# A decoder layer's weight products, 256 columns a matmul: one order of three products for each gate/up group

## Chip, cores and metric

One NeuronCore of a Trainium2 chip. The metric is the device time of one launch in microseconds (us), from first to last instruction with what little lies around them; lower is better.

## What is computed

A hybrid decoder layer on a residual stream h of 256 tokens by 2048 columns in float32. Every norm is an RMS norm with a gain, except the layer norm in the convolution.

```python
h = h + 0.5 * rms(swiglu(rms(h), w_gu[2048, 11264], w_down[5632, 2048]))      # FFN 1
z = rms(h) @ w_in[2048, 5120]                                                  # conv a, g; q, k, v
h = h + rms(concat(conv_group(a, g), moba_attention(q, k, v)) @ w_out)         # token mixing
h = h + rms(cross_attention(rms(h), rms(mem)))                                 # 4 heads, 256 memory rows
h = h + 0.5 * rms(swiglu(rms(h), w_gu, w_down))                                # FFN 2
```

With 256 tokens there is one MoBA block, so the attention is causal attention inside it.

## The kernel before

**Three products.** TensorE multiplies in float32r, a type of reduced precision. To keep float32 accuracy, each operand is split in two float32r parts, hi and lo, with value = hi + lo. A weight product w·x is then the sum of three matmuls that accumulate in PSUM: hi·xh, hi·xl and lo·xh. `Weights` (lines 96 to 220) loads weight tiles of 128 x 1024 on SP's DMA queue (4 buffers), makes hi on ScalarE (ACT, line 177 or 179, 4 buffers) and lo on VectorE (DVE, line 193 or 195, 3 buffers), ahead of use. `step` (line 318) issues this work for later tiles, then the matmuls of one tile, then pieces of `Background` work. All engine orders are the order of issue in the program; nothing is reordered later.

**Two layouts of a product.** In `proj_T` (line 418) the weights are the stationary operand, 128 of their columns for each load, and 256 tokens stream past them. A *region* is 256 columns of a PSUM bank, half a bank. In `proj` (line 429) 128 tokens are stationary and 512 weight columns stream, into a whole bank. Every matmul carries a weight load of its own, also where the same stationary operand comes twice running.

**Gate and up** (`gate_up`, line 622). A feed-forward layer has 22 groups g of 256 gate and 256 up columns; a group is 8 steps u, each one weight tile of two k-tiles (k = 2u + e) of the contraction. Groups 0 and 1 (`few`) use `proj_T`: 4 regions in 2 banks; for each k, hi·xh and hi·xl of region after region, then lo·xh of all four: 12 matmuls of 256 columns. The other 20 groups join the first two products: `xk` holds xh and xl side by side, so one matmul of 512 columns gives both partial sums in the two halves of a bank, and a matmul of 256 adds lo·xh to the second half:

```python
for ps, w in zip(pss, ws):
    nc.tensor.matmul(ps, hi[:, w], xk, start=k == 0, ...)             # L637, 512 columns, 4 banks
for ps, w in zip(pss, ws):
    nc.tensor.matmul(ps[:, 256:512], lo[:, w], xk[:, 0, :], ...)      # L639, 256 columns
```

That is 8 matmuls a k-tile, 4 banks a group. `queue_gate` (line 585) then queues background pieces: ACT copies one half of each bank (line 597) and DVE adds the other (line 598), for gate and for up; then the scale by 1/rms, silu, product, and the split of the result into hi and lo for the down product.

**Down** (line 483): two halves of the output columns, 44 k-tiles each, for each 2 token halves x 2 banks x 3 products with `proj` (lines 434, 436, 438), 512 columns each. The last 3 tiles of the second half are held back and done bank by bank. The output projection of the token mixing is the same function with 16 k-tiles. `in_group` (q, k) and `glu_group` (convolution) use `proj_T`, the v columns `proj`. The memory values (lines 1078 to 1080) have an own loop, with tokens stationary and 256 columns: per region xh·hi, xl·hi, xh·lo. During the token mixing DVE and GpSimd (POOL) also compute the 31 taps of the convolution (lines 747 and 758).

Of the kernel before, what the change touches and what calls it, by code (L numbers as in the profile page):

```python
# [14 lines left out]
P = 128  # L15
# [27 lines left out]
class Background:  # L43
    """Work that is issued a piece at a time between the weight tiles."""

# [12 lines left out]
    def urgent(self, pieces):  # L58
        """Each of the pieces in a step of its own, before all else that waits."""
        for fn, dve, act in reversed(pieces):  # L60
            self.main.appendleft(None)
            self.main.appendleft((fn, dve, act, 0.0))
# [33 lines left out]
class Weights:  # L96
    """The weights in the order of their use: loads, then the two float32r parts, ahead of the products."""

# [21 lines left out]
    def start(self):  # L120
        """The first rows and weights, in halves."""
        for i in range(2):
            self.raw[i] = self.pool.tile([P, 1024], F32, name="raw", bufs=RAW)
        for i, e in ((0, 0), (1, 0), (1, 1), (0, 1)):
            c = slice(e * 512, (e + 1) * 512)
            self.nc.sync.dma_start(self.raw[i][:, c], self.entries[i][0][:, c])
        key = self.entries[0][2]
        self.chunks[key] = c = self.chunk()
        self.hi[key], self.lo[key] = c[:, :, 0, :], c[:, :, 1, :]
        self.hi[1] = self.pool.tile([P, 1024], F32R, name="hi", bufs=HI)  # L130
        self.lo[1] = self.pool.tile([P, 1024], F32R, name="lo", bufs=LO)
        for i, e in ((0, 0), (1, 0), (1, 1), (0, 1)):
            k = i if i else key
            src, hi, g = list(self.parts(i, self.hi[k]))[e]
            lo = list(self.parts(i, self.lo[k]))[e][1]
            if g is None:
                self.nc.scalar.activation(hi, src, AF.Copy)
                self.nc.vector.tensor_tensor(lo, src, hi.bitcast(F32), ALU.subtract)
            else:
                self.nc.scalar.activation(hi, src, AF.Copy, scale=g)  # L140
                self.nc.vector.scalar_tensor_tensor(lo, src, g, hi.bitcast(F32), ALU.mult, ALU.subtract)
        self.raw.pop(0)
        self.raw.pop(1)
        self.n_raw = self.n_hi = self.n_lo = 2

    def parts(self, i, whole):
        """The pieces of an entry that have a gain each: (raw, part of the tile, gain)."""
        _, gains, _, rows, _ = self.entries[i]
# [75 lines left out]
def layer_kernel(ctx: ExitStack, tc: tile.TileContext, x, mem, eye, consts, smalls, post_g, xt, memt,  # L224
# [12 lines left out]
    def tmp():  # L237
        return ap.tile([P, 512], F32, name="tmp", bufs=TMP)
# [84 lines left out]

# [1 line left out]
    def rsqrt_of(ssq, n, eps_col, scale):  # L325
# [26 lines left out]
    class Rows:  # L352
        """Transposed float32r parts of [256, 2048] rows, and their 1 / rms."""

# [62 lines left out]

    def proj_T(regions, first, last, hi, lo, xk, parts_first=False):
        order = [(f, r) for f in range(2) for r in enumerate(regions)]
        if not parts_first:  # L420
            order = [(f, r) for r in enumerate(regions) for f in range(2)]
        for f, (j, (ps, o)) in order:
            nc.tensor.matmul(ps[:, o:o + 256], hi[:, j * P:(j + 1) * P], xk[:, f, :],  # L423
                             start=first and o == 0 and f == 0, stop=False, skip_group_check=True)
        for j, (ps, o) in enumerate(regions):
            nc.tensor.matmul(ps[:, o:o + 256], lo[:, j * P:(j + 1) * P], xk[:, 0, :],  # L426
                             start=False, stop=last, skip_group_check=True)

    def proj(pss, first, last, hi, lo, xk, t, n0=0):
        xh = xk[:, 0, t * P:(t + 1) * P]  # L430
        xl = xk[:, 1, t * P:(t + 1) * P]
        cols = [slice((n0 + n) * 512, (n0 + n + 1) * 512) for n in range(len(pss))]
        for ps, c in zip(pss, cols):
            nc.tensor.matmul(ps, xh, hi[:, c], start=first, stop=False)  # L434
        for ps, c in zip(pss, cols):
            nc.tensor.matmul(ps, xl, hi[:, c], start=False, stop=False)  # L436
        for ps, c in zip(pss, cols):
            nc.tensor.matmul(ps, xh, lo[:, c], start=False, stop=last)  # L438

# [3 lines left out]
    class Post:  # L443
        """Post-norm of [256, 2048] products and the update of the residual stream."""

# [20 lines left out]
        def early(self, t):  # L466
            """The sum over all but the last columns, as the bias of the square root."""
            s1 = scal()
            nc.vector.reduce_sum(s1, self.ssq[t][:, 0:3], axis=AX.X)
            self.bias = scal()  # L470
            nc.vector.tensor_scalar(self.bias, s1, self.factor / D, self.factor * RMS_EPS, ALU.mult, ALU.add)
# [11 lines left out]
    def down(nk, lhs, post, hook=None, tail=TAIL, keep=False):  # L483
        """Columns in two halves; the last tiles of the second go through the tokens one half after the other."""
        for hf in range(2):
# [3 lines left out]
            def mm(k, hi, lo):  # L489
                if hf == 1 and k >= nk - tail:  # L490
                    held.append((k, hi, lo))
                    return
                for t in range(2):
                    proj(pss[t], k == 0, k == nk - 1, hi, lo, lhs(k), t)

# [29 lines left out]
    def boundary(post, last, rows, fillers):  # L525
        """From the last products of the second token half to the first transposed columns of the next phase."""
        fillers = deque(fillers)
# [57 lines left out]
    def queue_gate(G, U, rows, hi_, lo_):  # L585
        """A pair of banks has the two partial sums of 128 columns in each, a single one the sums of 256."""
        box = []

        def add_parts(pss):
            s = tmp()  # L590
            box.append(s)
            if len(pss) == 1:
                nc.scalar.copy(s, pss[0])
                return
            for i, ps in enumerate(pss):
                c = slice(i * 256, (i + 1) * 256)
                nc.scalar.copy(s[:, c], ps[:, 256:512])  # L597
                nc.vector.tensor_tensor(s[:, c], ps[:, 0:256], s[:, c], ALU.add)  # L598

        def gate():  # L600
            add_parts(G)
            nc.vector.tensor_tensor(two(box[0]), two(box[0]), bc2(rows.rb), ALU.mult)

# [4 lines left out]
        def product():  # L608
            nc.vector.tensor_tensor(box[0], box[0], box[1], ALU.mult)
            make_hi(hi_, two(box[0]))  # L610

        bg.add(gate, dve=1.3, act=0.8)
        bg.cut()
        bg.add(silu, act=0.5, pool=1.2)
        bg.add(lambda: add_parts(U), dve=0.7, act=0.8)
        bg.cut()
# [5 lines left out]
    def gate_up(rows):  # L622
        hT = []
        for g in range(2 * NG):
            few = g < 2
            pss = [bank() for _ in range(2 if few else 4)]

            def mm(u, hi, lo):
                for e in range(2):
                    k = 2 * u + e  # L630
                    xk = rows.x(k)
                    if few:
                        proj_T(regions_of(pss), k == 0, k == KT - 1, hi[:, e * 512:], lo[:, e * 512:], xk, g == k == 0)
                        continue
                    ws = [slice(e * 512 + j * P, e * 512 + (j + 1) * P) for j in range(4)]
                    for ps, w in zip(pss, ws):
                        nc.tensor.matmul(ps, hi[:, w], xk, start=k == 0, stop=False, skip_group_check=True)  # L637
                    for ps, w in zip(pss, ws):
                        nc.tensor.matmul(ps[:, 256:512], lo[:, w], xk[:, 0, :], start=False, stop=k == KT - 1,  # L639
                                         skip_group_check=True)  # L640

# [4 lines left out]
            c = slice(2 * (g % 2), 2 * (g % 2) + 2)  # L646
            queue_gate(pss[:len(pss) // 2], pss[len(pss) // 2:], rows, hT[-1][:, c, 0, :], hT[-1][:, c, 1, :])
        return hT
# [16 lines left out]

# [1 line left out]
    mem_rows = []  # L667
# [13 lines left out]
    def kv_k(half):  # L681
        """Four pieces, one for each quarter of the contraction."""
        box = []
# [14 lines left out]

# [1 line left out]
    rows = Rows(h_rows, "x")  # L700
# [19 lines left out]

# [1 line left out]
    rows = Rows(h_rows)  # L722
# [287 lines left out]

# [1 line left out]
    rows = Rows(h_rows)  # L1012
# [132 lines left out]

# [1 line left out]
    bg.add(lambda: rows.tr(1, 1))  # L1147
# [110 lines left out]
```

## Time and profile before

| what | value |
|---|---|
| median of the two timed runs | 1979.92 us (1978.13 and 1981.71) |
| span of the profiled execution, first to last instruction | 1979.2 us |
| TensorE matmul busy | 1925.5 us, 97%, 11,034 matmuls |
| VectorE, ScalarE, GpSimd busy | 64%, 56%, 10% |
| mean granted TensorE clock | 0.997 |

The page gives the profiled execution's span; it lies between the two runs. PE is TensorE's matmuls, PEld its weight loads. A matmul's recorded duration holds the time that it spends in the array behind others, so the pace of a stream is read from the distance of the starts.

### The profile page before, as it was taken

What the parts mean: (1) busy time and instruction counts of PE and PEld (TensorE: products, weight loads), DVE (VectorE), ACT (ScalarE), POOL (GpSimd) and SP (SyncE); (2) the same over time, 40 slices, a digit from 0 to 9 for tenths busy, and PEclk for the clock granted to TensorE, in tenths of its full rate; (3) what the DMA queues carried; (4) which work ended last, traced back from release to release, by engine and by line L of the source; (5) the groups of instructions that cost most, each with busy time, mean ns of one, the idle gap of its engine ahead of it and who ended that gap; (6) DMA issues with size and microseconds to landing.
All of it is one profiled execution on the core that took longest, in us unless ns stands there. A gap on an engine that the chain in (4) does not pass through costs nothing.

```text
span 1979.2 us, 29214 instructions
## 1 busy us (share of the span) xinstructions
PE 1925.5 (97%) x11034; PEld 1675.8 (85%) x11034; DVE 1268.0 (64%) x1774; ACT 1098.7 (56%) x1793; POOL 204.8 (10%) x192
## 2 busy tenths in 40 slices
PE   8999999999999999887899999999999999999998
PEld 8888888888888889886797898988888888888886
DVE  5666666666544556999767576666666666644444
ACT  6655555555434646766465565755555555533433
POOL 0000000000000000768401000000000000000000
PEclk9999999999999999999999999999999999999999
DMA  8666666666655774344555653566666666666664
GB/s 289 187 190 191 191 192 190 189 189 192 210 191 187 256 244 141 130 149 139 166 165 169 214 179 120 181 191 191 188 189 191 191 191 192 212 188 187 189 189 142
DMA packets 102094, 369.62 MB, mean 187 GB/s; under 512 B 11456, under 2 KB 11712, under 8 KB 101184
## 3 DMA queue, kind: packets, MB, share of 16 engines
q1 hardware_dynamic: 100944, 361.00, 58.5%
q10 hardware_dynamic: 1008, 6.75, 0.9%
q8 instruction: 86, 1.41, 0.3%
q14 instruction: 56, 0.46, 0.1%
HBM read 365.61 MB, written 2.10 MB: 186 GB/s over the span
## 4 chain that ended last, share of the span: by engine, by line
PE 89%; DVE 6%; issue 2%; POOL 2%; ACT 1%; DMA 1%; SPq 0%; DVEq 0%; POOLq 0%; ACTq 0%
PE ps L637 30%; PE ps L639 15%; PE ps L438 11%; PE ps L434 10%; PE ps L436 10%; PE ps L423 7%; PE ps L426 3%; DVE lo L195 3%; DVE cv L747 2%; POOL cv L758 1%; PE ps L339 0%; DMA raw<-in_f_gu_dram 0%; ACT hi L179 0%; PE ps L1080 0%; PE ps L1078 0%
## 5 line engine op out<-in xcount | busy, mean ns | idle before, releaser
L195 DVE SCALAR_TENSOR_TENSOR lo<-raw,sm,hi 128x512 fp32r<-128x512 f32 (+1 forms) x830 | 636.4, 806 | 335.1 <-issue 249.3
L179 ACT ACTIVATE hi<-raw,sm 128x512 fp32r<-128x512 f32 (+1 forms) x830 | 576.4, 741 | 374.8 <-PE ps L637 220.9
L637 PE MATMUL ps<-ck,hi 128*128 128x512 f32 x2560 | 693.4, 393 | 0.0
L637 PEld LDWEIGHTS ps<-ck,hi 128*128 128x128 f32 x2560 | 434.5, 188 | 55.0
L193 DVE TENSOR_TENSOR lo<-raw,hi 128x1024 fp32r<-128x1024 f32 x216 | 265.4, 1230 | 282.4 <-PE ps L438 248.6
L639 PEld LDWEIGHTS ps<-ck,lo 128*128 128x128 f32 x2560 | 388.0, 188 | 53.8
L639 PE MATMUL ps<-ck,lo 128*128 128x256 f32 x2560 | 399.5, 278 | 0.0
L177 ACT ACTIVATE hi<-raw 128x1024 fp32r<-128x1024 f32 x216 | 228.7, 1060 | 297.2 <-PE ps L436 253.0
L438 PE MATMUL ps<-lo,ck 128*128 128x512 f32 x896 | 286.6, 397 | 9.1 <-DVE lo L195 7.8
L434 PE MATMUL ps<-hi,ck 128*128 128x512 f32 x896 | 286.7, 397 | 1.0 <-ACT ck L347 1.0
L436 PE MATMUL ps<-hi,ck 128*128 128x512 f32 x896 | 285.2, 396 | 0.0
L423 PE MATMUL ps<-ck,hi 128*128 128x256 f32 x1664 | 229.3, 283 | 9.5 <-ACT hi L140 6.2
L423 PEld LDWEIGHTS ps<-ck,hi 128*128 128x128 f32 x1664 | 210.2, 189 | 10.6 <-ACT hi L140 6.2
L438 PEld LDWEIGHTS ps<-lo,ck 128*128 128x128 f32 x896 | 168.1, 188 | 53.5 <-DVE lo L195 10.9
L436 PEld LDWEIGHTS ps<-hi,ck 128*128 128x128 f32 x896 | 168.3, 188 | 41.8 <-DVE ck L350 0.4
L434 PEld LDWEIGHTS ps<-hi,ck 128*128 128x128 f32 x896 | 168.0, 188 | 41.6 <-ACT ck L347 1.2
L606 POOL TENSOR_TENSOR tmp<-tmp,rb 128x512 f32<-128x512 f32 x44 | 58.2, 1322 | 1125.1 <-ACT tmp L605 1105.8
L426 PE MATMUL ps<-ck,lo 128*128 128x256 f32 x832 | 129.4, 283 | 23.3 <-DVE lo L195 23.3
L426 PEld LDWEIGHTS ps<-ck,lo 128*128 128x128 f32 x832 | 110.5, 188 | 28.3 <-DVE lo L195 28.2
L758 POOL TENSOR_TENSOR cv<-cv,cf 128x255 f32<-128x255 f32 (+14 forms) x120 | 106.3, 887 | 31.9 <-ACT cf L757 23.7
L747 DVE SCALAR_TENSOR_TENSOR cv<-yv,cf,cv 128x255 f32<-128x255 f32 (+14 forms) x120 | 85.1, 709 | 2.7
L598 DVE TENSOR_TENSOR tmp<-ps,tmp 128x256 f32<-128x256 f32 x160 | 60.1, 417 | 10.2 <-ACT tmp L597 10.2
(142 smaller groups left out, 925.8 us busy)
## 6 DMA issues: line engine op xcount, KB each, us to landing
raw<-in_f_gu_dram SPq DMA_DIRECT2D x351, 512.0 KB, 4.1
raw<-in_f_down_dram SPq DMA_DIRECT2D x176, 512.0 KB, 4.3
raw<-in_w_in_dram SPq DMA_DIRECT2D x80, 512.0 KB, 3.6
raw<-in_w_out_dram SPq DMA_DIRECT2D x32, 512.0 KB, 3.6
cf<-in_post_g_dram ACTq DMA_DIRECT2D x4, 1024.0 KB, 6.9
raw<-in_x_k_dram SPq DMA_DIRECT2D x8, 512.0 KB, 3.9
raw<-in_x_q_dram SPq DMA_DIRECT2D x8, 512.0 KB, 4.3
raw<-in_x_o_dram SPq DMA_DIRECT2D x8, 512.0 KB, 4.3
```

Of the source, the lines that this page charges most:

```text
L177: self.nc.scalar.activation(dst, src, AF.Copy)
L179: self.nc.scalar.activation(dst, src, AF.Copy, scale=g)
L193: self.nc.vector.tensor_tensor(dst, src, hi.bitcast(F32), ALU.subtract)
L195: self.nc.vector.scalar_tensor_tensor(dst, src, g, hi.bitcast(F32), ALU.mult, ALU.subtract)
L423: nc.tensor.matmul(ps[:, o:o + 256], hi[:, j * P:(j + 1) * P], xk[:, f, :], start=first and o == 0 and f == 0, stop=False, skip_group_chec ...
L426: nc.tensor.matmul(ps[:, o:o + 256], lo[:, j * P:(j + 1) * P], xk[:, 0, :], start=False, stop=last, skip_group_check=True)
L434: nc.tensor.matmul(ps, xh, hi[:, c], start=first, stop=False)
L436: nc.tensor.matmul(ps, xl, hi[:, c], start=False, stop=False)
L438: nc.tensor.matmul(ps, xh, lo[:, c], start=False, stop=last)
L637: nc.tensor.matmul(ps, hi[:, w], xk, start=k == 0, stop=False, skip_group_check=True)
L639: nc.tensor.matmul(ps[:, 256:512], lo[:, w], xk[:, 0, :], start=False, stop=k == KT - 1, skip_group_check=True)
L758: nc.gpsimd.tensor_tensor(cv[:, ct, s:], cv[:, ct, s:], pr[:, :S - s], ALU.add)
```

## The change

All products that were 512 columns wide become two of 256, the two partial sums of a gate/up group are accumulated in one region, and the order of the three products depends on the group's number (g % 11) or, in the down product, on the k-tile (k // 8 % 4). Groups with g % 11 = 6 (groups 6 and 17 of each feed-forward layer) go in 128 columns. The doc strings are removed as well. The order also changes where no mode is given: `proj_T` now does hi·xh, hi·xl, lo·xh region by region, where all lo·xh came last.

```diff
+    def proj_T(regions, first, last, hi, lo, xk, parts_first=False, mode=0):
+        rs = list(enumerate(regions))
+        order = [(r, i) for r in rs for i in range(3)]
+        if parts_first:
+            order = [(r, i) for i in range(3) for r in rs]
+        elif mode == 2:
+            order = [(r, i) for r in rs for i in (0, 2, 1)]
+        elif mode == 3:
+            order = [(rs[j], i) for j in (0, 2, 1, 3) for i in range(3)]
+        elif mode == 4:
+            order = [(rs[j + e], i) for j in (0, 2) for i in range(3) for e in range(2)]
+        elif mode == 5:
+            order = [(rs[j + e], i) for j in (0, 1) for i in range(3) for e in (0, 2)]
+        elif mode == 6:
+            for j, (ps, o) in rs:
+                for h in (0, 128):
+                    for i in range(3):
+                        nc.tensor.matmul(ps[:, o + h:o + h + 128], (hi, hi, lo)[i][:, j * P:(j + 1) * P],
+                                         xk[:, i % 2, h:h + 128], start=first and o == 0 and i == 0 and h == 0,
+                                         stop=last and i == 2, skip_group_check=True)
+            return
+        elif mode == 7:
+            order = [(r, i) for i in (0, 1) for r in rs] + [(r, 2) for r in rs[::-1]]
+        elif mode == 8:
+            order = [(r, i) for r in rs for i in range(2)] + [(r, 2) for r in rs[::-1]]
+        for (j, (ps, o)), i in order:
+            nc.tensor.matmul(ps[:, o:o + 256], (hi, hi, lo)[i][:, j * P:(j + 1) * P], xk[:, i % 2, :],
+                             start=first and o == 0 and i == 0, stop=last and i == 2, skip_group_check=True)
+
+    def proj(pss, first, last, hi, lo, xk, t, n0=0, mode=0):
+        xs = [xk[:, f, t * P:(t + 1) * P] for f in (0, 1, 0)]
+        if mode in (2, 3):
+            for n, ps in enumerate(pss):
+                for i, w in enumerate((hi, hi, lo)):
+                    for o in (0, 256):
...
+            return
+        for n, ps in enumerate(pss):
+            for o in (0, 256):
+                c = slice((n0 + n) * 512 + o, (n0 + n) * 512 + o + 256)
+                for i, w in enumerate((hi, hi, lo)):
+                    nc.tensor.matmul(ps[:, o:o + 256], xs[i], w[:, c], start=first and o == 0 and i == 0,
+                                     stop=last and i == 2, skip_group_check=True)
...
-                    proj(pss[t], k == 0, k == nk - 1, hi, lo, lhs(k), t)
+                    proj(pss[t], k == 0, k == nk - 1, hi, lo, lhs(k), t, mode=k // 8 % 4)
...
         def gate():
-            add_parts(G)
-            nc.vector.tensor_tensor(two(box[0]), two(box[0]), bc2(rows.rb), ALU.mult)
+            box.append(tmp())
+            nc.vector.tensor_tensor(two(box[0]), two(G), bc2(rows.rb), ALU.mult)
...
         def product():
-            nc.vector.tensor_tensor(box[0], box[0], box[1], ALU.mult)
+            nc.vector.tensor_tensor(box[0], box[0], U, ALU.mult)
...
-            few = g < 2
-            pss = [bank() for _ in range(2 if few else 4)]
+            pss = [bank() for _ in range(2)]
 
             def mm(u, hi, lo):
+                if g % 11 == 9 and u:
+                    for j, r in enumerate(regions_of(pss)):
+                        for e in range(2):
+                            k = 2 * u + e
+                            proj_T([r], k == 0, k == KT - 1, hi[:, e * 512 + j * P:], lo[:, e * 512 + j * P:], rows.x(k))
+                    return
                 for e in range(2):
                     k = 2 * u + e
...
+                    proj_T(regions_of(pss), k == 0, k == KT - 1, hi[:, e * 512:], lo[:, e * 512:], rows.x(k),
+                           g == k == 0, g % 11)
```

## Rows read from the trace of the kernel before

**Rows 1.** The page: span, busy time of each engine, TensorE's clock by slices.
```profile
span 1979.2 us, 29214 instructions
...
PE 1925.5 (97%) x11034; PEld 1675.8 (85%) x11034; DVE 1268.0 (64%) x1774; ACT 1098.7 (56%) x1793; POOL 204.8 (10%) x192
...
PEclk9999999999999999999999999999999999999999
```

**Rows 2.** Table by stretch: gate/up of FFN 1, its down, the convolution's stretch.
```profile
core 0: us, PE busy (x) PEld busy (x) DVE busy (x) ACT busy (x) POOL busy (x), PEclk, DMA share, GB/s
...
57.00:500.00 443.00, 443.00 (x2563) 388.54 (x2562) 291.19 (x457) 258.48 (x440) 27.93 (x21) 1.00 0.64 191
500.00:748.00 248.00, 248.00 (x1071) 199.39 (x1070) 126.88 (x135) 116.47 (x152) 1.30 (x1) 1.00 0.66 213
840.00:935.00 95.00, 77.78 (x593) 72.51 (x594) 93.44 (x109) 64.29 (x111) 72.72 (x78) 1.00 0.46 141
```

**Rows 3.** Chain of waits, 65 to 81 us, a wide gate/up group: start, us, what.
```profile
65.35 0.93 PE ps L637 x4
...
79.19 0.93 PE ps L637 x4
```

**Rows 4.** Chain of waits, 1270 to 1281 us, a narrow (few) gate/up group.
```profile
1270.44 0.94 PE ps L423 x8
...
1278.92 0.94 PE ps L423 x8
```

**Rows 5.** Chain of waits, 500 to 540 us, down product.
```profile
500.19 0.47 PE ps L436 x2
...
537.99 0.47 PE ps L436 x2
```

**Rows 6.** PE's timeline, 1195 to 1206 us: memory values, transposes: start, us, engine, line.
```profile
1194.79 0.28 PE L1078 MATMUL ps<-hi,ck 128*128 128x256 f32 x1
...
1197.06 0.28 PE L1080 MATMUL ps<-lo,ck 128*128 128x256 f32 x1
1197.17 0.60 PE L1051 MATMUL ps<-ident,cf 128*128 128x128 f32 x4
```

**Rows 7.** PE and PEld groups by line and shape: count, busy us, mean ns.
```profile
L637 PE MATMUL ps<-ck,hi 128*128 128x512 f32 x2560 | 693.4, 393 | 0.0
...
L423 PE MATMUL ps<-ck,hi 128*128 128x256 f32 x1664 | 229.3, 283 | 9.5 <-ACT hi L140 6.2 <-ACT hi L179 2.6 <-ACT ck L347 0.7
...
L1051 PE MATMUL ps<-ident,cf 128*128 128x128 f32 x16 | 2.4, 272 | 0.0
...
L423 PEld LDWEIGHTS ps<-ck,hi 128*128 128x128 f32 x1664 | 210.2, 189 | 10.6 <-ACT hi L140 6.2 <-ACT hi L179 2.8 <-ACT ck L347 0.9
...
L1051 PEld LDWEIGHTS ps<-ident,cf 128*128 128x128 f32 x16 | 1.8, 140 | 0.0
```

**Rows 8.** PE's timeline at 1052 us: one plain float32 product of 128 columns.
```profile
1052.12 0.39 PE L836 MATMUL ps<-cf 128*128 128x128 f32 x2
```

**Rows 9.** DVE and ACT groups, 57 to 500 us: the joining of the partial sums.
```profile
L598 DVE TENSOR_TENSOR tmp<-ps,tmp 128x256 f32<-128x256 f32 x76 | 28.6, 417 | 4.9 <-ACT tmp L597 4.9
...
L597 ACT COPY tmp<-ps 128x256 f32<-128x256 f32 x76 | 23.7, 360 | 0.0
```

**Rows 10.** Waits of PE, 755 to 1070 us: for whom, us in total, times, longest.
```profile
PE ps L426 <- DVE lo L195: 23.3, 24, 1.5
PE ps L438 <- DVE lo L195: 7.8, 6, 3.1
```

**Rows 11.** Chain of waits, 840 to 935 us: where it passes from DVE to PE.
```profile
869.75 1.66 DVE lo L195
871.40 0.04 issue
871.45 1.21 PE ps L426 x8
...
908.64 1.65 DVE lo L195
...
912.64 1.64 DVE lo L195
```

More of the change, by code (lines that the diff above doesn't have):

```diff
@@ L416, in h_rows @@
         return h[:, t, c * 512:(c + 1) * 512]
[L418 to L438, printed above, removed]
+    def proj_T(regions, first, last, hi, lo, xk, parts_first=False, mode=0):
[26 more added lines that the diff above has]
+                             start=first and o == 0 and i == 0, stop=last and i == 2, skip_group_check=True)
@@ new lines, in proj @@
+    def proj(pss, first, last, hi, lo, xk, t, n0=0, mode=0):
[10 more added lines that the diff above has]
+            for o in (0, 256):
+                c = slice((n0 + n) * 512 + o, (n0 + n) * 512 + o + 256)
+                for i, w in enumerate((hi, hi, lo)):
+                    nc.tensor.matmul(ps[:, o:o + 256], xs[i], w[:, c], start=first and o == 0 and i == 0,
+                                     stop=last and i == 2, skip_group_check=True)
@@ L587, in queue_gate @@
         box = []
[L589 to L598, printed above, removed]
         def gate():
-            add_parts(G)
-            nc.vector.tensor_tensor(two(box[0]), two(box[0]), bc2(rows.rb), ALU.mult)
+            box.append(tmp())
+            nc.vector.tensor_tensor(two(box[0]), two(G), bc2(rows.rb), ALU.mult)
         def silu():
@@ L608, in product @@
         def product():
-            nc.vector.tensor_tensor(box[0], box[0], box[1], ALU.mult)
+            nc.vector.tensor_tensor(box[0], box[0], U, ALU.mult)
             make_hi(hi_, two(box[0]))
-        bg.add(gate, dve=1.3, act=0.8)
+        bg.add(gate, dve=0.7)
         bg.cut()
         bg.add(silu, act=0.5, pool=1.2)
-        bg.add(lambda: add_parts(U), dve=0.7, act=0.8)
         bg.cut()
@@ L624, in gate_up @@
         for g in range(2 * NG):
-            few = g < 2
-            pss = [bank() for _ in range(2 if few else 4)]
+            pss = [bank() for _ in range(2)]
             def mm(u, hi, lo):
+                if g % 11 == 9 and u:
[4 more added lines that the diff above has]
+                    return
                 for e in range(2):
                     k = 2 * u + e
[L631 to L640, printed above, removed]
+                    proj_T(regions_of(pss), k == 0, k == KT - 1, hi[:, e * 512:], lo[:, e * 512:], rows.x(k),
+                           g == k == 0, g % 11)
             for u in range(8):
@@ L646, in gate_up @@
             c = slice(2 * (g % 2), 2 * (g % 2) + 2)
-            queue_gate(pss[:len(pss) // 2], pss[len(pss) // 2:], rows, hT[-1][:, c, 0, :], hT[-1][:, c, 1, :])
+            queue_gate(pss[0], pss[1], rows, hT[-1][:, c, 0, :], hT[-1][:, c, 1, :])
         return hT
```

## The prediction

> **What bounds the kernel now.** I read the page first. TensorE is busy for 1925.5 of 1979.2 us, VectorE for 64% and ScalarE for 56% [rows 1], and TensorE's clock stands at its upper level, 2.4 GHz, in every slice. So TensorE is the bound almost everywhere, and the question is what one matmul costs it. The table by stretch says where that doesn't hold: in gate/up and down PE is busy for the whole stretch, but from 840 to 935 us DVE is (93.4 of 95 us) and PE only for 77.8 [rows 2]. A busy PE says nothing of its pace, so I took the pace of each kind of stream from the distance between starts, in the chain of waits and in PE's timeline:
>
> - A wide gate/up group: the same piece of the chain starts at 65.35 and, five steps of two k-tiles later, at 79.19 us: 13.84 / 5 = 2.768 us a step [rows 3]. A step streams 24 x 256 columns, so 115.3 ns per 256 columns.
> - A narrow group (the first two, 256 columns a matmul): 8.48 us for six k-tiles of 12 matmuls, 117.8 ns a matmul [rows 4].
> - Down, 512 columns: 37.80 us for 27 rounds of six matmuls, 233.3 ns each, 116.7 per 256 columns [rows 5].
> - The memory values (tokens stationary, 256 columns, the three products of a region in a row): 20 starts from 1194.79 to 1197.06 us, 113.5 ns each [rows 6].
>
> So 256 columns cost between 113.5 and 117.8 ns in every stream, whatever the width of the matmul. At 2.4 GHz 256 columns alone are 106.7 ns. Each matmul has its own weight load: the counts of loads and matmuls are equal, 11,034 each [rows 1], also in the line that uses one stationary operand twice running (1,664 and 1,664) [rows 7]. At 256 columns the loads hide beside the streaming; the trace has no float32r product of fewer columns.
>
> **The change part by part.** The sum is made on the profiled execution's span, 1979.2 us, which lies 0.7 us below the median of the two timed runs (1979.92) and between them; I neglect that. The number of columns stays the same everywhere; what changes is in how many matmuls they come.
>
> *Groups 6 and 17, in 128 columns.* Four groups in all. A step has 2 k-tiles x 4 regions x 2 halves x 3 = 48 matmuls and 48 loads in place of 16. If only columns counted, one would take 113.5 / 2 = 57 ns; if the load is the pace, one can't be slower than a 256-column matmul with the same load, 118 ns. The nearest rows are the transposes: 128 columns and a load for each, four in a row in 0.60 us, of which the last one's own duration is 0.27, so (0.60 - 0.27) / 3 = 110 ns apart [rows 6, 7]. They stream half as many columns as the memory values and are hardly quicker, which looks like a load that sets the pace. The loads of float32r are recorded longer than theirs (189 against 140 ns), and still follow each other every 113.5 ns. I take 110. A step is 48 x 110 = 5.28 us instead of 2.768, that is +2.51 us, times 4 groups x 8 steps = 32: **+80.4 us**. Nothing hides it, since PE is busy there throughout. Bounds by the rows: 57 ns gives -1.0 us, 118 ns gives +92.7. Loads and splits for later tiles only get more time.
>
> The Trainium skill (TensorE: Matmul & The Clock Gate, "Back-to-back issue gap") speaks against so large a term: pairs of load and matmul shall sustain about 81 ns at 128 columns and 131 at 512. The trace doesn't bear the second figure out (233.3 ns [rows 5]), so I weigh the first little. By it the step would be 48 x 81 = 3.89 us and the term +35.9 in place of +80.4.
>
> *The other wide groups.* 2 x (20 - 2) = 36 groups, 288 steps, go from 16 matmuls to 24 of 256 columns. The nearest stream is that of the narrow groups, with the same operands: 24 x 117.8 = 2.827 us, +0.059 a step, **+17.0 us**. The other end is the pace of the memory values: 2.724 us a step, -12.7 us. The orders (modes 2 to 5, 7 to 9) lie somewhere between; no row tells them apart.
>
> *Down and the output projection.* Modes 0 and 1 have the very order of the memory values, with the same kinds of operand: 113.5 against 116.7 ns. Of the 512-column matmuls, 2 x 2 x 28 x 12 = 1344 in the feed-forward downs (k below 16 and from 32 on) and 2 x 16 x 12 = 384 in the output projection get this: 1728 x (233.3 - 227.0) = **-10.9 us**. The other 768 (modes 2 and 3) use one stationary operand twice running; I leave them at nothing, between -4.8 (at 227) and +1.8 us (at 235.6).
>
> *lo is needed sooner.* In `in_group` 16 matmuls ran before the first lo·xh, now two: 14 x 117.8 = 1.65 us less slack, in the v columns about 0.7. Where PE keeps pace this is covered, as lo is split two tiles ahead. From 840 to 935 us it isn't; between 755 and 1070 us PE waits for lo already, 30 times for 31.1 us [rows 10]. But the chain there runs in DVE, from one lo to the next in about 4.0 us [rows 11], against 2.83 us of matmuls, so waiting earlier costs nothing until the chain hands over to PE: at 871.45 us it continues with the 8 last lo products [rows 11], and will continue with 22 matmuls, 1.65 us more. Two such places: **+3 us**, between 0 and +8.
>
> *Gate without joining.* The copies and adds of halves go (76 of each in FFN 1's stretch, 23.7 us of ACT and 28.6 of DVE [rows 9]), and a group holds 2 banks, not 4. Neither engine is the bound there (DVE 291 of 443 us [rows 2]), so this gives nothing; it covers the change of order. DVE now reads gate and up from PSUM, in operations that it did before from SBUF, equally off the path.
>
> Sum: 80.4 + 17.0 - 10.9 + 3 = +89.5, **2069 us**. With the ends of the small terms and 109 to 118 ns for the narrow matmuls this case alone runs from about 2030 (+78.8 - 12.7 - 15.7) to 2102 us.
>
> **Rivals.**
> 1. *The array sets the pace in 128 columns as well* (the other side). Then a narrow matmul costs 57 ns, and the sum is -1.5 + 17.0 - 10.9 + 3, +8: 1987 us, no slower than can be measured. For it: no row shows a float32r load as a limit. Against: the transposes' 110 ns. The place is groups 6 and 17; below (39.6 - 9.1) / 32 = 0.95 us more a step, 78 ns a matmul, the change stays within 2%. Faster by over 2% it is only if the orders also run below every pace seen.
> 2. *A narrow product costs twice what I take*, because float32r in 128 columns is done as plain float32. A plain float32 product of 128 columns shows as two matmuls (0.39 - 0.27) = 0.12 us apart [rows 8], some 224 ns for the pair: 48 x 224 = 10.75 us a step, +255 us, 2244 us in all. For it: nothing in the kernel before is both float32r and narrower than 256. Against: plain float32 is two matmuls at 256 columns too, so type and not width decides.
> 3. *Waiting for lo becomes the path in the convolution's stretch.* If each of the 30 waits grew in full, 24 x 1.65 + 6 x 0.7 = 44 us come on top in place of 3: 2110 us. Against: after its lo PE needs 22 x 0.118 = 2.6 us of a DVE period of 4.0.
>
> **How the numbers follow.** The forecast has 0.75; rival 1 0.09; rival 2 0.11; rival 3 0.05. The range, 2020 to 2120 us, holds the forecast and rival 3; rivals 1 and 2 are left out. A measurement tells 2%, 39.6 us, from no change. Slower by more: the forecast, rivals 2 and 3, and 0.01 of rival 1, 0.92. Within: 0.06 of rival 1. Faster: its last 0.02.
>
> **What would show it.** PE has 11,034 + 2784 (each 512 of the tokens-stationary products split) + 36 x 16 x 4 + 4 x 16 x 16 = 17,146 matmuls. In the table by stretch group 6 should take some 42 us and its neighbours 22.6; starts in it 110 ns apart. A group 6 of 22 us is rival 1, of 86 us rival 2. Down should run at 113.5 ns where k is below 16, an unsplit group's neighbours at 117.8. The copies of halves are gone, PE's idle time is as before, and its waits for lo are longer but as many. The prediction is wrong if the narrow matmuls are under 100 or over 125 ns apart, or if orders differ by more than the 4 ns between the known paces.

## The result, and the profile after

| | us |
|---|---|
| before, median of 2 runs | 1979.92 (1978.13 to 1981.71) |
| after, median of 2 runs | 2083.83 (2080.97 to 2086.69) |
| after, profiled execution | 2080.97, span 2079.2 |
| ratio after to before | 1.0525, 95% interval 1.0505 to 1.0546 |

The change makes the kernel 5% slower; the forecast was 2069 us, the range 2020 to 2120.

The page, in the order of [rows 1]:

```profile
span 2079.2 us, 41201 instructions
...
PE 2026.0 (97%) x17146; PEld 2015.2 (97%) x17146; DVE 1214.4 (58%) x1614; ACT 1053.3 (51%) x1625; POOL 203.9 (10%) x192
...
PEclk9999999999999999999999999999999999999999
```

TensorE is still the bound and, slice by slice, still at its upper clock level (0.996 on average). There are 17,146 matmuls, as counted ahead, and as many loads. Weight loads are now busy for 97% of the span, against 85%: with fewer columns behind each load, there is almost no time without one.

The table by stretch, with the columns of [rows 2]. The stretches are gate/up group 3 of FFN 1, the narrow group 6, group 14 of FFN 1 and group 3 of FFN 2 (both in the order of group 3), FFN 1's down, and the convolution's stretch:

```profile
76.61:98.37 21.76, 21.76 (x195) 21.76 (x194) 13.32 (x19) 11.76 (x18) 1.30 (x1) 1.00 0.61 193
141.89:184.71 42.82, 42.82 (x386) 42.82 (x385) 13.11 (x19) 11.82 (x18) 1.27 (x1) 1.00 0.34 111
343.06:365.67 22.61, 22.61 (x194) 22.61 (x193) 13.21 (x19) 11.80 (x18) 1.29 (x1) 1.00 0.56 186
1351.71:1374.33 22.62, 22.62 (x195) 22.62 (x193) 13.21 (x19) 11.79 (x18) 1.30 (x1) 1.00 0.58 185
544.00:796.00 252.00, 252.00 (x2140) 251.95 (x2139) 126.56 (x132) 116.11 (x148) 1.29 (x1) 1.00 0.64 210
890.00:985.00 95.00, 78.20 (x614) 74.48 (x613) 93.51 (x110) 62.88 (x109) 71.16 (x76) 0.98 0.45 144
```

Three things are to be seen. The narrow group takes 42.8 us, where groups 5 and 7 beside it take 21.8 and 22.7; DVE and ACT do the same work in it, and the DMA share falls from 0.6 to 0.34, so it is TensorE alone that needs the time. Groups 3 and 14 have the same order of the three products and the same 192 matmuls, yet differ by 0.85 us; the same group 3 in FFN 2 differs from itself in FFN 1. And the convolution's stretch looks as it did: DVE 93.5 of 95 us, PE 78.

The paces come from the chain of waits, as before: start, us, what, and how many matmuls. Group 3, group 6, groups 9 to 11, FFN 1's down (lines 463 and 456 are two of its orders), the output projection of the mixing, and that of the attention:

```profile
75.97 22.10 PE ps L445 x195
...
142.05 42.83 PE ps L436 x384
...
251.94 24.15 PE ps L445 x205
...
559.94 29.68 PE ps L463 x252
589.62 10.48 PE ps L456 x89
...
1129.96 40.12 PE ps L463 x354
...
1257.92 12.12 PE ps L463 x101
```

By division: 113.3 ns a matmul in group 3; 42.83 us / 384 = 111.5 ns in the narrow group; 117.8 ns in groups 9 to 11; 117.8 in down, in both orders; 113.3 in one output projection and 120.0 in the other.

Stage by stage, from each stage's first matmul to the next's, in the traces of both kernels: gate/up 1 537.4 against 493.4 us (+44.1), gate/up 2 541.7 against 490.0 (+51.7), the downs 252.05 against 249.7 and 248.6 against 246.2 (+4.8), the output projection 100.3 against 101.15 (-0.8), the stages of the mixing before it -1.1, the attention's output projection +1.2. This adds up to the difference of the spans, 100 us, but for 0.1. Gate/up 2 loses 7.6 us more than gate/up 1: its groups 2 to 5 ran at 117.8 ns instead of 113.3 (3.4 us), and its groups 0 and 1 took 1.5 us more than in before, where those of FFN 1 took 2.6 less. The granted clock was 0.66 from 1280 to 1285 us, where gate/up 2 starts, and 1.00 at the same place in before (1234 to 1239 us).

### The profile page after: what moved, and what is told of

Its sections match the earlier page's. It is cut to its first block, busy times and chain, and to the rows that moved or that the text cites. A ratio compares the mean times of both kernels' runs of the same rounds, so it can differ in the third digit from the quotient of the medians.

```text
span 2079.2 us, 41201 instructions
## 1 busy us (share of the span) xinstructions
PE 2026.0 (97%) x17146; PEld 2015.2 (97%) x17146; DVE 1214.4 (58%) x1614; ACT 1053.3 (51%) x1625; POOL 203.9 (10%) x192
## 4 chain that ended last, share of the span: by engine, by line
PE 89%; DVE 5%; issue 2%; POOL 1%; ACT 1%; DMA 1%; SPq 0%; DVEq 0%; POOLq 0%; ACTq 0%
PE ps L445 49%; PE ps L463 21%; PE ps L456 9%; PE ps L436 8%; DVE lo L195 3%; DVE cv L757 2%; POOL cv L768 1%; DMA raw<-in_f_gu_dram 1%; PE ps L339 0%; ACT hi L179 0%; PE ps L1090 0%; PE ps L1088 0%; PE ps L1089 0%; DVE h L506 0%; DVE lo L193 0%
## 5 line engine op out<-in xcount | busy, mean ns | idle before, releaser
L445 PE MATMUL ps<-ck,hi 128*128 128x256 f32 x6272 | 1054.4, 280 | 8.0 <-ACT hi L140 6.8
L445 PEld LDWEIGHTS ps<-ck,hi 128*128 128x128 f32 x6272 | 915.2, 188 | 9.1 <-ACT hi L140 6.8
L445 PE MATMUL ps<-ck,lo 128*128 128x256 f32 x3136 | 775.4, 281 | 24.1 <-DVE lo L195 24.1
L445 PEld LDWEIGHTS ps<-ck,lo 128*128 128x128 f32 x3136 | 545.6, 189 | 29.0 <-DVE lo L195 29.0
L463 PE MATMUL ps<-hi,ck 128*128 128x256 f32 x2560 | 453.0, 281 | 1.3 <-ACT ck L347 1.0
L463 PEld LDWEIGHTS ps<-hi,ck 128*128 128x128 f32 x2560 | 392.7, 190 | 2.0 <-ACT ck L347 1.2
L463 PE MATMUL ps<-lo,ck 128*128 128x256 f32 x1280 | 360.1, 281 | 9.0 <-DVE lo L195 7.1
L463 PEld LDWEIGHTS ps<-lo,ck 128*128 128x128 f32 x1280 | 241.6, 189 | 10.6 <-DVE lo L195 8.4
L436 PE MATMUL ps<-ck,hi 128*128 128x128 f32 x1024 | 171.5, 275 | 0.0
L456 PE MATMUL ps<-hi,ck 128*128 128x256 f32 x1024 | 162.6, 281 | 0.0
L436 PEld LDWEIGHTS ps<-ck,hi 128*128 128x128 f32 x1024 | 155.5, 192 | 0.0
L436 PE MATMUL ps<-ck,lo 128*128 128x128 f32 x512 | 140.9, 275 | 0.0
L456 PEld LDWEIGHTS ps<-hi,ck 128*128 128x128 f32 x1024 | 139.4, 190 | 0.1
L456 PE MATMUL ps<-lo,ck 128*128 128x256 f32 x512 | 102.0, 281 | 0.0
L436 PEld LDWEIGHTS ps<-ck,lo 128*128 128x128 f32 x512 | 98.3, 192 | 0.0
```

The costliest lines, as they stand in the source:

```text
L436: nc.tensor.matmul(ps[:, o + h:o + h + 128], (hi, hi, lo)[i][:, j * P:(j + 1) * P], xk[:, i % 2, h:h + 128], start=first and o == 0 and i ...
L445: nc.tensor.matmul(ps[:, o:o + 256], (hi, hi, lo)[i][:, j * P:(j + 1) * P], xk[:, i % 2, :], start=first and o == 0 and i == 0, stop=last ...
L456: nc.tensor.matmul(ps[:, o:o + 256], xs[i], w[:, c], start=first and o == 0 and i == 0, stop=last and i == 2, skip_group_check=True)
L463: nc.tensor.matmul(ps[:, o:o + 256], xs[i], w[:, c], start=first and o == 0 and i == 0, stop=last and i == 2, skip_group_check=True)
```

## The experiments

**Without the narrow groups.** Groups 6 and 17 get the default order in 256 columns, the rest stays as after.

```diff
-                           g == k == 0, g % 11)
+                           g == k == 0, 0 if g % 11 == 6 else g % 11)
```

> The changed kernel with groups 6 and 17 in 256 columns too. Theory (pace kept from what came before): the narrow groups give back 4 x (42.8 - 22.6) = 81 us, and since nothing interrupts the stream after group 1, groups 6 to 21 of FFN 1 and its first down half keep the pace of groups 1 to 5; at 113.3 ns that is another 15 to 20 us, so about 1985 us, at 117.8 ns 2003 us. Rival (the order of the products sets the pace): 2003 us, groups 1 to 5 at 113.3 ns and groups 7 to 10 at 117.8 ns again.

Measured: 1995.33 us (1993.26 to 2002.59), ratio to before 1.0086, interval 1.0063 to 1.0109. So without the four narrow groups 2083.8 - 1995.3 = 88 us of the 104 are gone. By themselves they cost 4 x (42.83 - 22.61) = 81. The rest is the net of changes in stretches whose code was not touched. In the chain of waits, gate/up of FFN 1, then FFN 1's down and FFN 2's:

```profile
199.95 40.16 PE ps L445 x341
...
559.99 35.47 PE ps L456 x313
595.47 4.65 PE ps L463 x41
...
1799.90 26.97 PE ps L456 x229
1826.87 13.19 PE ps L463 x112
```

FFN 1's down now runs at 113.3 ns a matmul (it ran at 117.8 in after) and takes 243.45 us in place of 252.05; FFN 2's stays at 117.8. And all gate/up groups from 2 on run at 117.8, also those that ran at 113.3. The same instructions have two paces. Neither expectation held: with every order at 117.8 ns in both layers, the order doesn't set the pace, and down didn't keep the pace of the gate/up ahead of it.

**The narrow groups alone.** Before, with groups 6 and 17 in 128 columns and nothing else.

```diff
+            narrow = g % 11 == 6
+            pss = [bank() for _ in range(2 if few or narrow else 4)]
...
+                    if narrow:
+                        for j, (ps, o) in enumerate(regions_of(pss)):
+                            for c in (0, 128):
+                                for i in range(3):
+                                    nc.tensor.matmul(ps[:, o + c:o + c + 128], (hi, hi, lo)[i][:, ws[j]],
+                                                     xk[:, i % 2, c:c + 128],
...
```

> The kernel before with only groups 6 and 17 in 128 columns (512-column matmuls everywhere else). If the narrow groups are the cost by themselves, each takes 42.8 us in place of 22.1, +83 us, some 2063 us, with 111.5 ns between starts. If the cost depended on the 256-column streams around them, less.

Measured: 2062.96 us, 83 above before. In its chain of waits the narrow group stands among wide ones:

```profile
144.46 0.47 PE ps L649 x4
144.93 42.83 PE ps L641 x384
187.75 0.98 PE ps L647 x4
```

The same 42.83 us as in after, so the price depends neither on the neighbours' width nor on their pace.

**Other widths.** Group 6 comes in four matmuls of 64 columns, group 17 in one of 192 and one of 64 (as many loads as 128 + 128).

```diff
-                for h in (0, 128):
+                for h, n in cuts:
...
+                           [(0, 64), (64, 64), (128, 64), (192, 64)] if g < 11 else [(0, 192), (192, 64)])
```

> The changed kernel with group 6 in 64 columns a matmul and group 17 in 192 and 64 by turns. If the weight load sets the pace, starts are about 111 ns apart in both: group 6 takes 96 x 8 x 0.111 = 85 us and group 17 the same 42.8 us as with 128 and 128. If columns plus a fixed cost set it (111.5 = 57 + 55), group 6 takes 96 x 8 x 0.083 = 64 us, and group 17 shows two distances, some 140 and 83 ns.

Measured: 2304.91 us. Group 17, from the chain of waits:

```profile
535.61 42.80 PE ps L436 x384
```

192 + 64 columns take what 128 + 128 take, 111.5 ns on average. Columns with a fixed cost would give the same sum, so the single distances have to tell the two apart, in TensorE's timeline:

```profile
540.34 0.27 PE L436 MATMUL ps<-ck,lo 128*128 128x192 f32 x1
540.45 0.33 PE L436 MATMUL ps<-ck,hi 128*128 128x64 f32 x2
540.61 0.28 PE L436 MATMUL ps<-ck,lo 128*128 128x64 f32 x1
540.73 0.45 PE L436 MATMUL ps<-ck,hi 128*128 128x192 f32 x2
```

The last matmul of a run of three is followed after 0.11 us where it has 192 columns (540.34), and after 0.12 where it has 64 (540.61); columns with a fixed cost would make that 0.14 and 0.08. The single starts in the trace say the same: 111 to 115 ns in either width, and only behind the first matmul of each run 173 (192 columns) and 49 (64), together as much as two of the others. Group 6 agrees at first: 64 columns start 111.7 ns apart, as 128 do, and not the 83 of the rival. So the load, not the columns, sets the pace. The Trainium skill (TensorE: Matmul & The Clock Gate, "LDWEIGHTS (loading the stationary operand)") gives a load the number of stationary columns over 1.2 GHz, 106.7 ns for 128; 111.5 ns are 5% more.

Then group 6 shows something else, in TensorE's timeline:

```profile
147.46 0.39 PE L436 MATMUL ps<-ck,hi 128*128 128x64 f32 x2
...
150.81 0.39 PE L436 MATMUL ps<-ck,hi 128*128 128x64 f32 x2
...
151.20 0.61 PE L436 MATMUL ps<-ck,hi 128*128 128x64 f32 x2
...
152.48 0.61 PE L436 MATMUL ps<-ck,hi 128*128 128x64 f32 x2
```

From 147.46 to 150.81 us 30 matmuls start 111.7 ns apart, from 151.20 to 152.48 six start 213 ns apart. The table by stretch has the granted clock (the columns of [rows 2]):

```profile
143.00:150.00 7.00, 7.00 (x64) 7.00 (x62) 3.66 (x6) 2.67 (x4) 0.00 (x0) 1.00 0.51 170
...
200.00:300.00 100.00, 100.00 (x471) 100.00 (x470) 7.67 (x11) 6.67 (x10) 0.00 (x0) 0.50 0.08 27
322.00:340.00 18.00, 18.00 (x155) 18.00 (x154) 9.97 (x15) 8.67 (x14) 1.30 (x1) 1.00 0.52 179
```

The granted clock fell from 1.00 to 0.50 (1.2 GHz), while TensorE was busy without a gap, and came back once the stream had 256 columns again. The group took 160.2 us, where 85 were expected. Loads follow the clock: 471 matmuls in 100 us are 212 ns each. In 128 columns this did not happen; the clock of the narrow groups stands at 1.00 in after and in the run before this one.

**One order, different starts.** All gate/up groups have the default order in 256 columns; the first k-tile of group g begins with g // 2 + 1 matmuls that are split in two of 128.

```diff
-        for (j, (ps, o)), i in order:
+        for n, ((j, (ps, o)), i) in enumerate(order):
+            if n < cut:
+                for h in (0, 128):
+                    nc.tensor.matmul(ps[:, o + h:o + h + 128], (hi, hi, lo)[i][:, j * P:(j + 1) * P],
+                                     xk[:, i % 2, h:h + 128], start=first and o == 0 and i == 0 and h == 0,
...
-                           g == k == 0, g % 11)
+                           g == k == 0, 0, g // 2 + 1 if k == 0 else 0)
```

> The changed kernel, all groups in the default order (mode 0) and 256 columns, but in the first k-tile of group g the first g // 2 + 1 matmuls are split in two of 128 columns (1 to 11 of them, each count in two groups of each FFN). Theory (an interruption draws the pace anew, which is then kept): some groups run at 113.3 and some at 117.8 ns though all have the same order; if the count decides, all four groups with one count agree. Rival (order sets the pace): all groups alike, 117.8 ns. Time 1985 to 2010 us.

Measured: 2019.47 us, above the 1985 to 2010 expected, which set the price of the splits too low: five of them make a group 0.55 us longer at the same pace (22.31 against 21.76 us), so the 264 of this run cost some 29 us. What matters here are the groups' paces. From the chain of waits, groups 8, 10 and 13, each with the split matmuls (line 447) ahead:

```profile
192.35 1.07 PE ps L447 x10
193.42 21.25 PE ps L451 x187
...
236.98 1.29 PE ps L447 x12
238.27 21.96 PE ps L451 x186
...
306.00 1.51 PE ps L447 x14
307.52 21.02 PE ps L451 x185
```

With the very same order a group runs at 113.6 ns after five split matmuls, 118.1 after six, 113.6 after seven (divided by the 187, 186 and 185 matmuls in one piece). An even count was followed by the slower pace in all 20 groups that had one; after 5, 7 and 11 all twelve were at the faster pace; after 1, 3 and 9 there were some of each. So the order of the products is not what decides, and an interruption can switch the pace, which then holds for the rest of the group.

**Is it the count?** In gate/up only group 2 gets five split matmuls, to see whether the faster pace then lasts; in the downs every fourth k-tile begins with k // 4 + 1 split ones.

```diff
+                    m = 128 if cut > 0 else 256
+                    cut -= 1
+                    for h in range(o, o + 256, m):
...
+                    proj(pss[t], k == 0, k == nk - 1, hi, lo, lhs(k), t, cut=k // 4 + 1 if k % 4 == t == 0 else 0)
...
+                           g == k == 0, 0, 5 if g == 2 and k == 0 else 0)
```

> All in 256 columns and the default order. Group 2 of each FFN begins with five matmuls split in two, and in the down products (also the output projection) every fourth k-tile begins with n = k // 4 + 1 matmuls split. Theory (an odd count of split matmuls, three or more, leaves the stream at 113.3 ns, an even one at 117.8, and the pace is kept): groups 2 to 21 of both FFNs at 113.3 ns, 17 us less each than at 117.8, and in down the same rule by count in all four halves. Rival (the pace is drawn by chance): groups 2 to 21 change their pace between the two FFNs, and the same count gives different paces in the four halves. By the theory about 1970 us with the splits' own cost, by the rival 1965 to 2005.

Measured: 2020.46 us, outside both forecasts; 294 split matmuls at the 0.11 us of the run before make up some 32 us of it. In the chain of waits, gate/up and down of FFN 1:

```profile
199.98 40.04 PE ps L451 x340
...
559.96 40.09 PE ps L472 x354
```

Five split matmuls in group 2 were followed by 117.8 ns this time, up to the end of both gate/ups; the downs ran at 113.3 ns after every count from 1 to 11, in all four halves. Only the held-back tiles at the end of both downs, where nothing is split, went over to 117.8. So the count alone does not decide, and what does stays open.

**Down alone.** Before, with only `proj` as in after (256 columns, modes); gate/up stays at 512.

> The kernel before with the tokens-stationary products alone in 256 columns (gate/up as before). Theory: down runs at one of the two paces, 113.3 or 117.8 ns, from one interruption to the next, whatever the mode, so each of the downs takes between 240 and 249 us in place of 246 to 250, and the whole lies between 1962 and 1985 us. Rival (modes set the pace): k-tiles 0 to 15 and 32 to 43 differ from 16 to 31 in every half.

Measured: 1970.38 us beside 1978.43 of before on the same chip. Both downs at 113.3 ns, 243.0 and 239.6 us, 6.7 and 6.6 less than in before; after, with this very `proj`, needs 2.3 and 2.5 more. The 13.3 us are what the forecast's term gives if all four modes have the faster pace: (1344 + 768) x 6.3 ns. The output projection gives 0.8 us, the attention's takes 1.2 more, and the rest of the span took 2.3 us more in this run.

**Trying to set the faster pace.** No narrow groups; groups 2 to 5 begin with 5, 5, 7 and 11 split matmuls, each half of a down with one.

```diff
-                           g == k == 0, g % 11)
+                           g == k == 0, 0, {2: 5, 3: 5, 4: 7, 5: 11}.get(g, 0) if k == 0 else 0)
```

> All in 256 columns and the default order; groups 2, 3, 4 and 5 of each FFN begin with 5, 5, 7 and 11 matmuls split in two, and each half of a down product with one. If odd counts draw the quick pace in gate/up as in the map by groups, and one split does so in down as in the map of down, groups 6 to 21 run at 113.3 ns, a down takes some 242 us, and the whole takes 1950 to 1960 us. If the draw in gate/up goes the other way, both layers' groups at 117.8 ns, 1985 us; one layer each way, 1970.

Measured: 1992.45 us (1977.71 to 1994.23, nine runs), ratio 1.0056, interval 1.0038 to 1.0073. A miss: in the profile gate/up stayed at 117.8 ns, only the downs are at 113.3. But eight runs lie between 1990.67 and 1994.23 and one at 1977.71; that one was not profiled, so that one of its gate/ups had the faster pace (20 groups x 192 x 4.5 ns = 17 us) is a guess.

**Offset of the operands.** A tile of 64 bytes that nobody reads shifts the tokens' tiles against the weights' tiles, as the only edit, once in the kernel without narrow groups, once in before.

```diff
+    pad = ap.tile([P, 16], F32, name="pad")
+    nc.vector.memset(pad, 0.0)
```

> The kernel without narrow groups (a1), with one unused tile of 64 bytes that moves the tokens' tiles by 64 bytes against the weight tiles, so that both start at the same offset within 128 bytes. Where both operands lie in one pool already (held weights: the keys, the attention's output projection) 256 columns took 120 ns in the changed kernel. Theory (the relative offset of the two operands sets which paces a stream can have): 120 ns in nearly all groups and in down, about 2030 us. Rival (offset doesn't matter; what interrupted the stream before does): 113.3 and 117.8 ns as in a1, 1993 to 2003 us.

> The kernel before with the same unused tile of 64 bytes. Theory (offset): all 512-column products at 226.6 ns as in the attention's output projection, not 233.3, so a down takes 242 us in place of 246 to 250 and the output projection of the mixing 2.6 us less; lo products of gate/up at 120 in place of 115.5 ns, which takes back what the wide ones give there: about 1963 us. Rival (offset doesn't matter): 1980 us, no difference.

Measured: 2020.46 us in 256 columns, 25 more than without the shift. The two clean paces are gone; starts in gate/up lie 115 to 122 ns apart, 118.7 on average, which is down's average too. Of the 25 us, 10.5 are FFN 1's down, which had the faster pace without the shift. In before 1992.62 us (1991.27 to 1995.3), ratio 1.0066, interval 1.0054 to 1.0078. Two lines of its chain of waits, 27 k-tiles apart in the same group kind as [rows 3]:

```profile
60.42 0.93 PE ps L640 x4
...
98.34 0.93 PE ps L640 x4
```

37.92 / 27 = 1.404 us a k-tile, against 1.384 in before [rows 3]: 117.0 ns per 256 columns for 115.3. Over 40 groups of 16 k-tiles that is 13 us; the spans differ by 11.6. The downs got quicker, by 1.0 us each: 15 rounds of six matmuls lie between the next two lines, 232.3 ns a matmul for 233.3 [rows 5].

```profile
563.73 0.47 PE ps L441 x2
...
584.64 0.47 PE ps L441 x2
```

So the place of the tiles matters to the pace, since nothing else differs in these streams, but not in one direction. My expectation for before had the sign wrong, so the rule that I had put behind it falls; how offset and pace hang together stays open.

**The versions that beat both.** Down alone once more, timed; and before with a `proj_half` of 256 columns in the default order in down and in the mixing's v columns, one split matmul at each half's start, and the attention's output projection left at 512.

```diff
-                    proj(pss[t], k == 0, k == nk - 1, hi, lo, lhs(k), t)
+                    proj_half(pss[t], k == 0, k == nk - 1, hi, lo, lhs(k), t, cut=1 if k == t == 0 else 0)
```

> The kernel of a7 (the tokens-stationary products alone in 256 columns, gate/up as before), now timed in rounds. If what leads into down draws its pace the same way in every run, down is at 113.3 ns each time and the ratio is 0.995, 1970 us. If the draw differs from run to run, times between 1969 and 1985 us and a ratio near 1.

> As a10, but in the default order, with one matmul split in two at the start of each half of a down product, and with the attention's output projection left at 512 columns (1.2 us less than in a7). If one split draws the quick pace in down whatever came before, as it did for all 44 splits there, 1967 to 1970 us in every run, a ratio of 0.994. If a10's draw is quick anyway, the two differ by the 1.2 us alone.

Measured: 1968.91 us (1966.09 to 1969.29), ratio 0.9942, interval 0.9929 to 0.9954, and 1967.71 us (1967.26 to 1970.79), ratio 0.9945, interval 0.9931 to 0.9958. The first one's chain of waits in FFN 1's down:

```profile
559.97 25.50 PE ps L437 x225
585.47 14.62 PE ps L444 x129
```

Both orders at 113.3 ns. The split matmul and the attention's 512 columns bring nothing that shows beside it: the two intervals cover each other. Half a per cent is gained by 256 columns where tokens are stationary; the loss of the change comes from gate/up, and a little of it from downs that ran at the slower pace.

## Why the prediction was right, and where not

- *Narrow groups, +80.4 us.* Right, and by its mechanism. The transposes' distance, 110 ns, stood for a load that sets the pace; 111.5 ns were measured, +82.8 us against the steps of before, and the distances behind 192 and 64 columns showed that the load is what counts. Rival 1, the array as the pace (57 ns), and rival 2, plain float32 (224 ns), are both out: there is one record for each of 17,146 matmuls, and one takes 111.5 ns. The Trainium skill's sustained 81 ns at 128 columns (TensorE: Matmul & The Clock Gate, "Back-to-back issue gap"), by which the term would have been +35.9, doesn't hold for this stream either.
- *Other wide groups, +17.0.* About right, by luck in part. 32 of the 36 ran at 117.8 ns as taken, groups 2 to 5 of FFN 1 at the other end, 113.3. Against the 8 x 2.768 = 22.14 us of before that is 4 x -0.38 + 32 x 0.48 = +14.
- *Down and output projection, -10.9.* The step that failed. It took the order of the products, "the very order of the memory values", as the reason for their 113.5 ns. The output projection did run at 113.3, but gave 0.8 us only, and both downs ran at 117.8 in modes 0 and 1 as in 2 and 3: about +4 in place of -10.9. Where down alone was changed, both downs did run at 113.3, and in the run without narrow groups FFN 1's did. A pace of this kind belongs to the stream as it happens to run, not to an order. The trace of before had a row that says so: in the attention's output projection the same lines in the same order, 512 columns wide, took 1.36 us for six matmuls, 226.7 ns each, where down took 233.3 [rows 5]:

```profile
1215.63 0.62 PE L434 MATMUL ps<-ck 128*128 128x512 f32 x2
...
1216.99 0.62 PE L434 MATMUL ps<-ck 128*128 128x512 f32 x2
```

  This term alone is 15 us off. On the profiled span the whole sum is 10.5 off (+100.0 for +89.5), as the errors of the others took back 4.5; so the forecast lies this near partly by luck.
- *lo sooner, +3.* Nothing of it shows; off the path, as rival 3's counter-argument had it. TensorE's waits, 800 to 1120 us, answer to [rows 10]:

```profile
PE ps L445 <- DVE lo L195: 23.9, 23, 2.0
PE ps L463 <- DVE lo L195: 7.1, 5, 3.2
PE ps L463 <- DVE lo L193: 1.8, 2, 1.3
```

  32.8 us in 30 waits, against 32.3 in 32 in before (to the 31.1 us of [rows 10] come two waits of line 438 for the lo of line 193, 1.2 us); the stages came out 1.1 us shorter. So the waits are neither longer nor fewer to speak of. The hand-over of [rows 11] was read too short: in before the chain didn't leave TensorE after the 8 lo products at 871.45 us, but went on with 16 and 8 more matmuls, 4.16 us in all. Two lines from there, and the same place in after:

```profile
872.65 1.88 PE ps L423 x16
...
878.04 0.88 ACT cf L757 x2
```

```profile
917.02 1.66 DVE lo L195
918.72 4.14 PE ps L445 x21
...
925.31 0.88 ACT cf L767 x2
```

  From lo (869.75 [rows 11] and 917.02) to that piece of ACT 8.29 us pass in both, so the hand-over cost nothing. TensorE's 21 matmuls took as long as the 32 of before, because the granted clock was 0.50 from 919.6 to 923 us; what they would have taken at the upper level isn't shown.
- *Gate without joining, 0.* Right. The rows of [rows 9] have no successors; DVE reads both sums from PSUM, off the path, as it is busy for 13 of 22 us in a group.
- *The orders.* The sign of being wrong, orders further apart than the known paces, did not show (113.3 and 117.8 ns were the ends again), but for another reason: nothing that was seen belongs to an order. In after both paces occur in one order (groups 3 and 14), the one-order kernel shows both, and without the narrow groups all orders of gate/up ran at 117.8 ns.
- *Two readings.* Not every stream of before lay between 113.5 and 117.8 ns: the key products at 746.39 us, with 256 columns, started 119 ns apart. And rival 1 takes -1.5 us for the 57 ns that gave -1.0 above; nothing hangs on it.

The two runs of after lie 5.7 us apart, those of before 3.6. Draws of the pace could explain that of after, but its second run has no trace, so this is not shown.

## What to carry to other kernels

Read the pace of a matmul stream from the distance between starts, and ask what each start needs: here every matmul brings its own 128-column load, and 128 columns behind one leave TensorE waiting for loads (111.5 ns), so that halving 256 nearly doubles the stage. Before an order of instructions is called faster, run one order in several places and one place in several orders: two paces 4% apart appeared here in identical code. Narrower pieces may still pay where the load doesn't set the pace: 256 for 512 columns in the stages with stationary tokens took 0.6% off the whole time, as these streams then ran at the faster pace. Why they did is open, and 512 columns had it too in one place (226.7 ns).

## What the runs showed of the hardware that was not expected

- A stream of 256-column matmuls of float32r holds 113.3 or 117.8 ns for hundreds of matmuls, and an interruption (a narrow group, a few split matmuls) can switch it. What decides which, neither the order nor the number of split matmuls alone, stays open.
- 64 bytes of shift between the tiles of the two operands changed the pace of every long stream: in before gate/up went from 115.3 to 117.0 ns per 256 columns and down from 233.3 to 232.3 per 512, 0.7% on the whole; in 256 columns all went to 118.7, by one run.
- TensorE's granted clock can fall to half in a stretch without any idle time: in 64-column matmuls it did, and their starts went from 111.7 to 213 ns.
